# 128-row score passes, exchanged ends of SBUF in the second part, and scalings ordered behind low parts, in a one-core decoder layer

## The chip, the cores and the metric

The kernel runs on 1 core of one Trainium2 chip. Inputs are laid in device memory and one program is launched. The metric is the device time of that program in microseconds (us), the median of several runs. The core's engines are called as in the profile: PE (TensorE, matrix products), PEld (its weight loads), DVE (VectorE), ACT (ScalarE), POOL (GpSimd) and SP (SyncE, which here issues nearly all DMAs).

## The reference

One pre-norm layer over 2048 positions of width 1024, all in float32:

```python
h = rms_norm(x, norm1_g)
proj = h @ w_in                                   # 1024 -> 768 + 1792 columns
q, ka, va = split(proj[..., :768])                # 8 heads of 64; 2 key/value heads
r, k, v, wd, ad, gd = split(token_shift(proj[..., 768:], shift_mu))
att = sliding_window_attention(q, ka, va, sinks)  # window 128, blocks of 128, ALiBi
rw = rwkv7_time_mix(r, k, v, wd, ad, gd, ...)     # 8 heads, recurrent state 64x64 each
x = x + concat([att, rw], -1) @ w_out
h = rms_norm(x, norm2_g)
u = causal_depthwise_conv3(h @ w_gate)            # 1024 -> 2816
x = x + (silu(u) * (h @ w_up)) @ w_down
out = rms_norm(x, final_g)
```

In the attention a block of 128 queries sees the 256 keys of its own block and the one before it: `s = q k^T * 64**-0.5`, minus the slope times the distance, masked, and a softmax with a sink logit per head.

## The kernel before, in words

Every product of two float32 matrices is made of passes in a narrower format (F32R): each operand is split into a high part, copied by ACT, and a low part, which is the operand minus that copy (made by POOL or DVE). `mm3` then issues three passes: high by high, high by low, low by high.

**The first part** (`with ExitStack() as A`) works in 4 blocks of 512 positions and in 4 pairs of heads per block: 16 units, numbered n. One turn of the main loop does several stages for different units at once: `t_prep` and the projections of unit n+2, `t_x` of unit n+1, `chain` (the recurrence) and `t_attn` of unit n, and `t_out` of unit n-1. All PE, ACT and DVE instructions of this part are issued in the order in which the program names them (`in_order`); that order comes from a planner (`tick`, `defer`, `run_until`) with costs and positions in the table `Q`. POOL's and SP's orders are the scheduler's after the first turns.

For `t_x`, a triangular system is solved: `px` makes products on PE, `XB` masks them on DVE, `inv_in` sends them through device memory (`dL`) and back in another layout (`LL`), `subst` makes 31 steps of two DVE instructions each (`Mt` and `M`, woven one at a time between other DVE instructions), `inv_out` brings the result back (`dT`, `TT`), and `merge0` to `merge2` finish it on DVE and PE (`T`, `ph`).

The keys of a block are projected in `ak_done`: ACT writes the high part of each key head g into its own 64 partitions of `kTh`, DVE writes the low part into `kTl` (64 partitions for each head, 128 together), and POOL copies the high part to the other 64 partitions, so that `kTh[:, g]` holds the head's high part twice. A query tile `q{g}` holds the query's high part in one half of the partitions and its low part in the other. In `scores(q2, g)` each of two query blocks has two passes into one PSUM region of 128 by 256:

```python
mm(out=pS[:, e, w0:], lhsT=qg[:, qs], rhs=kTh[:, g, kks]..., start=True, stop=False)
mm(out=pS[:, e, w0:], lhsT=qg[gs, qs], rhs=kTl[gs, kks]..., start=False, stop=True)
```

The first reads 128 partitions, the second 64. There are 4 such calls in each of the 16 units, 64 in all. Each call is followed by the softmax on DVE and ACT (`P`), a transpose on PE (`pT`) and the product with the values (`pO`).

`pw_` makes the decay: one running sum on DVE over 512 positions (`scan`, with the mask `rmask` that starts it again every 64), then exponentials on ACT, of which `E` is used in `writes` one turn later and, in its last column of each chunk, in `chain` two turns later. There are 3 buffers of E.

**The second part** (`with ExitStack() as B`) is traced without that order, but for its first stage. It has three stages:

- O: the output projection (`o_job`, 20 jobs of 24 matmuls), with `cat_load`/`cat_split` for its inputs and `wo_part` for its weights, then the second normalisation, the transposes (`o_tr`) and the operands h2 of the next stage (`combos`). Tiles `r` hold the transposes of positions 1024 and up until they are stored to `h1raw`.
- F: gate and up products in 22 pairs, by a seven-product scheme on 2 by 2 blocks (`quad`, products 1, 6, 7, 5, 2, 4, 3). `unit` splits each weight combination into `uh` and `ul`, six buffers each.
- D: the down product by the same scheme, product by product (`ORDER` 1, 2, 6, 7, 4, 5, 3), 11 steps k of 24 matmuls each. Each step takes three units: two of activations (`ul_a`, low part on POOL) and one of weights (`ul_b`, low part on DVE). `residual` adds x on POOL, `square` sums squares on ACT, `scale_of` makes the factor `rso` on POOL, and `finish` scales and stores: half of the results on DVE while product 3 runs, in its steps k below 8, together with a POOL product `c11 * fgb`.

**Memory.** Pools are stacked from the two ends of each partition of SBUF, in the order in which they are opened; a closed pool gives its bytes to the next on its side, and a tile of the new pool waits until the tiles whose bytes it takes are done, DMAs that read them included. The first tile of a name takes the lowest buffer, the next ones the highest and then downwards. The addresses of the kernel before, in bytes of a partition: first part, constants 928 to 44,800 (with `lgh`, `lgl` at 5,248 to 9,344), operands h 44,800 to 93,952, projection weights to 126,720, scratch `tp` 130,944 to 163,648 (three buffers `t`, which hold `xr`, from 139,136), `pp` to 210,752, attention to 229,248. Second part: from the left `fwp` (three buffers `st` for all loads) 1,504 to 13,792, `rw` 15,072 to 37,600, `op` 37,600 to 111,456 (cath, catl, woh and wol, xn, xt, r), and in their place later `units` 15,072 to 43,744, `fgp`, `hp2`; from the right `h2` 114,656 to 229,344. D's pool `fdp` begins on the left at 43,744.

Of the kernel before, what the change touches and what calls it, by code (L numbers as in the profile page):

```python
# [10 lines left out]
F32 = mybir.dt.float32  # L11
# [72 lines left out]
def hybrid_trunk_kernel(  # L84
# [112 lines left out]
    with ExitStack() as A:  # L197
# [84 lines left out]
        cent = acon.tile([P, P], F32, name="cent")  # L282
        rmask = acon.tile([P, NCH, C], mybir.dt.bfloat16, name="rmask")
        cmask = acon.tile([P, 2, C], mybir.dt.bfloat16, name="cmask")
        cmb = cmask.rearrange("p s t -> p (s t)").unsqueeze(1)
        bias = acon.tile([P, 256], mybir.dt.bfloat16, name="bias")
        kTh = acon.tile([P, 2, 5, P], F32R, name="kTh")
        kTl = acon.tile([P, 5, P], F32R, name="kTl")
        vth = acon.tile([P, 5, P], F32R, name="vth")
        vtl = acon.tile([P, 5, P], F32R, name="vtl")  # L290
        NE = 3
        Es = [acon.tile([P, NCH, C + 1], F32, name=f"E{i}") for i in range(NE)]
# [295 lines left out]
        def t_kv(F, b):  # L588
            def ak_done(ps):
                if b > 0:  # L590
                    gcopy(out=kTh[:, :, 0], in_=f32(kTh[:, :, 4]))
                    gcopy(out=kTl[:, 0], in_=f32(kTl[:, 4]))
                H["kb"] = b
                kh = kTh[:, :, 1:].rearrange("p g n t -> p g (n t)")
                kl = kTl[:, 1:].rearrange("p n t -> p (n t)")
# [24 lines left out]

            return {"ak": ak_done, "av": av_done}, vtr


# [3 lines left out]
        def t_prep(F, n):  # L627
# [4 lines left out]
            S = U[n] = {}  # L632
            E = S["E"] = Es[n % NE]

            def k_done(ps):
# [38 lines left out]
            def pw_():  # L674
# [9 lines left out]
                def go1():  # L684
                    scan(out=sw, data0=rmask.rearrange("p c t -> p (c t)"), data1=sw, initial=0.0, op0=ALU.mult, op1=ALU.add)
# [48 lines left out]
        def t_x(F, n):  # L734
# [84 lines left out]
            def subst():  # L819
                M, LL = S["M"], S["LL"]  # L820
                for i in range(31):
# [61 lines left out]
        def chain(n, fill):  # L883
            b, j = divmod(n, NPAIR)
            u = f"{b}_{j}"
            S = U[n]
            W, SV, XB, Bt, IK, TT, E = S["W"], S["SV"], S["XB"], S["Bt"], S["IK"], S["TT"], S["E"]
# [105 lines left out]
        def t_attn(n):  # L993
# [6 lines left out]
            def scores(q2, g):  # L1000
                def go():
# [13 lines left out]
                    for e in range(2):  # L1015
# [5 lines left out]
                           start=True, stop=False)  # L1021
                        mm(out=pS[:, e, w0:], lhsT=qg[gs, qs], rhs=kTl[gs, kks].rearrange("p n t -> p (n t)"),
                           start=False, stop=True)
# [220 lines left out]
    with ExitStack() as B:  # L1244
        bc = B.enter_context(tc.tile_pool(name="bc", bufs=1, reuse_waits="tile"))
        wp = B.enter_context(tc.tile_pool(name="fwp", bufs=2, reuse_waits="tile"))
        ps_b = B.enter_context(tc.tile_pool(name="ps_b", bufs=8, space=PSUM, reuse_waits="tile"))
        sp_ = B.enter_context(tc.tile_pool(name="fsp", bufs=1, reuse_waits="tile"))
        G = ExitStack()
        h2 = G.enter_context(tc.tile_pool(name="h2", bufs=1, side="right", reuse_waits="tile"))  # L1250

# [3 lines left out]
        def gsub(out, in0, in1):  # L1255
            nc.gpsimd.tensor_tensor(out=out, in0=in0, in1=in1, op=ALU.subtract)  # L1256

# [17 lines left out]
        O = ExitStack()  # L1275
        rw = O.enter_context(tc.tile_pool(name="rw", bufs=1, reuse_waits="tile"))
        op_ = O.enter_context(tc.tile_pool(name="op", bufs=1, reuse_waits="tile"))
        b11, b12 = (h2.tile([P, 4, 512], F32, tag=f"{c}3", name=n) for c, n in (("h", "b11"), ("l", "b12")))
# [170 lines left out]
        F = ExitStack()  # L1449
        up_ = B.enter_context(tc.tile_pool(name="units", bufs=1, reuse_waits="tile"))  # L1450
        gp = F.enter_context(tc.tile_pool(name="fgp", bufs=1, reuse_waits="tile"))
        hp2 = F.enter_context(tc.tile_pool(name="hp2", bufs=1, reuse_waits="tile"))
        NPR = NF // 2
        actc = {p: [dpool.tile([P, NHALF, 512], F32, name=f"actc_{p}_{k}") for k in range(NPR)] for p in PRODS}

        def unit(src, name, lo=gsub, shape=None):
# [6 lines left out]
            act(h_, src, AF.Copy)  # L1463
            lo(l_, src, f32(h_))
            return hi, lw

        def vsub(out, in0, in1):
            nc.vector.tensor_tensor(out=out, in0=in0, in1=in1, op=ALU.subtract)  # L1468

# [263 lines left out]
        def scale_of(j, m):  # L1733
            i = tok[j][m]
            ms = MS[i]
            rs = sp_.tile([P, 1], F32, tag="rso", name=f"rso_{i}", bufs=8)
            gts(out=rs, in0=ms[0], scalar1=ms[1], scalar2=RMS_EPS, op0=ALU.add, op1=ALU.add)
            gtt(out=rs, in0=rs, in1=mhalf[:, 0:1], op=ALU.pow)
            return rs

        def finish(j, m, e, c, rs, scaled=False):
            es = slice(512 * e, 512 * e + 512)
            if scaled:
                act(c, c, AF.Copy, scale=rs)
            else:
                stt(out=c, in0=c, scalar=rs, in1=fgb[:, es], op0=ALU.mult, op1=ALU.mult)
            nc.sync.dma_start(out=out_t[tok[j][m]][:, es], in_=c)
# [5 lines left out]
        for p in ORDER:  # L1753
# [3 lines left out]
            for k in range(NPR):  # L1757
# [76 lines left out]
```

## Time and profile before

| | us |
|---|---|
| median of 3 runs (lowest, highest) | 2703.64 (2700.2, 2708.16) |
| the profiled execution, its time | 2707.62 |
| its span | 2705.9 |
| PE busy in the span | 2568.1 (95%) |
| DVE, POOL, ACT busy | 1722.6, 1461.2, 1284.7 |

The span is from the first to the last instruction of the profiled execution. A busy PE is not PE at its peak, since matmuls are pipelined: the step from the start of one matmul to the start of the next says more than the duration of either. By the names of the tiles the first part ends at about 1244 us, stage O at 1404, stage F at 2261.

### The profile page before, as it was taken

How to read it: one execution, taken by the hardware profiler on the slowest of the kernel's cores; microseconds unless marked ns; L12 is line 12 of the kernel's file. 1: busy time of each engine (PE TensorE's matmuls, PEld its weight loads, DVE VectorE, ACT ScalarE, POOL GpSimd, SP SyncE). 2: the span in 40 equal slices, each digit the busy share in tenths (PEclk: the TensorE clock that was granted, in tenths of full speed). 3: DMA queues.
4: the chain of work that ended last, by engine and by line, in shares of the span. 5: the costliest groups of instructions: out<-in, count | busy, mean ns of one | idle time of the engine just before them, and what ended most of it. 6: DMA issues, size and time to landing. Idle time of an engine off the chain costs nothing.

```text
span 2705.9 us, 42161 instructions
## 1 busy us (share of the span) xinstructions
PE 2568.1 (95%) x15211; PEld 1998.0 (74%) x15211; DVE 1722.6 (64%) x3217; ACT 1284.7 (47%) x2737; POOL 1461.2 (54%) x1356
## 2 busy tenths in 40 slices
PE   7799999999999999998989999999999999999997
PEld 5566766677667766676768788787888888878885
DVE  6577767767677757743756777767676675443343
ACT  5356655655566655643434433345334333343343
POOL 6334443444344434321647778768666665484594
PEclk9899999989999999998999999999999999999998
DMA  4222222222223222335662434545233336742354
GB/s 129 64 63 73 73 73 73 71 59 71 66 64 96 65 65 73 85 110 173 190 206 92 155 135 153 162 165 174 94 98 110 108 113 236 231 141 95 112 176 147
DMA packets 333108, 313.94 MB, mean 116 GB/s; under 512 B 102576, under 2 KB 254274, under 8 KB 332898
## 3 DMA queue, kind: packets, MB, share of 16 engines
q1 hardware_dynamic: 332290, 310.71, 37.3%
q8 instruction: 119, 1.95, 0.3%
q14 instruction: 91, 0.75, 0.1%
q10 hardware_dynamic: 608, 0.53, 0.1%
HBM read 229.26 MB, written 81.92 MB: 115 GB/s over the span
## 4 chain that ended last, share of the span: by engine, by line
PE 63%; DVE 17%; DMA 6%; POOL 5%; issue 5%; ACT 4%; SPq 0%; POOLq 0%; ACTq 0%; DVEq 0%
PE d L104 14%; PE q_g L104 14%; PE q_u L104 12%; DVE M L124 4%; DVE Mt L124 4%; PE poa L104 3%; PE pin_q L104 2%; DMA LL<-dL 2%; PE px L104 2%; PE pc L104 2%; PE pin_k L104 2%; DVE P L124 2%; PE po L104 2%; PE ph L104 1%; PE pS L104 1%
## 5 line engine op out<-in xcount | busy, mean ns | idle before, releaser
L1256 POOL TENSOR_TENSOR ul_a<-sa,uh_a 128x512 fp32r<-128x512 f32 x154 | 208.8, 1361 | 154.6 <-ACT uh_a L110 153.9
L1256 POOL TENSOR_TENSOR ul_u<-s_u,uh_u 128x512 fp32r<-128x512 f32 x154 | 217.2, 1419 | 138.6 <-ACT uh_u L110 138.5
L1256 POOL TENSOR_TENSOR ul_g<-s_g,uh_g 128x512 fp32r<-128x512 f32 x154 | 220.3, 1439 | 56.0 <-ACT uh_g L110 55.9
L104 PE MATMUL q_g<-h2h,uh_g 128*128 128x512 f32 x616 | 242.6, 394 | 6.5 <-DVE u_g L1471 5.9
L104 PE MATMUL q_u<-h2h,uh_u 128*128 128x512 f32 x616 | 240.2, 390 | 2.5 <-DVE ct L1471 2.2
L104 PE MATMUL q_g<-h2l,uh_g 128*128 128x512 f32 x616 | 241.6, 392 | 0.0
L104 PE MATMUL q_g<-h2h,ul_g 128*128 128x512 f32 x616 | 241.3, 392 | 0.3 <-POOL ul_g L1256 0.3
L104 PE MATMUL q_u<-h2h,ul_u 128*128 128x512 f32 x616 | 239.9, 389 | 1.0 <-POOL ul_u L1256 1.0
L104 PE MATMUL q_u<-h2l,uh_u 128*128 128x512 f32 x616 | 239.7, 389 | 0.0
L104 PE MATMUL d<-ul_b,uh_a 128*128 128x512 f32 x616 | 232.4, 391 | 6.7 <-DVE ul_b L1468 6.7
L104 PE MATMUL d<-uh_b,ul_a 128*128 128x512 f32 x616 | 227.5, 391 | 3.5 <-POOL ul_a L1256 3.5
L110 ACT ACTIVATE uh_a<-sa 128x512 fp32r<-128x512 f32 x154 | 97.2, 631 | 235.6 <-PE d L104 128.3
L104 PE MATMUL d<-uh_b,uh_a 128*128 128x512 f32 x616 | 204.1, 389 | 0.0
L110 ACT ACTIVATE uh_u<-s_u 128x512 fp32r<-128x512 f32 x154 | 95.1, 628 | 222.4 <-DVE s_u L1468 116.8
L1468 DVE TENSOR_TENSOR ul_b<-wd,uh_b 128x512 fp32r<-128x512 f32 x55 | 68.1, 1239 | 189.2 <-ACT uh_b L110 183.8
L124 DVE TENSOR_TENSOR Mt<-M,LL 128x60 f32<-128x60 f32 (+24 forms) x496 | 159.8, 322 | 36.8 <-DMA LL<-dL 28.3
L110 ACT ACTIVATE uh_g<-s_g 128x512 fp32r<-128x512 f32 x154 | 95.1, 629 | 185.3 <-PE q_u L104 100.9
L124 DVE TENSOR_TENSOR M<-M,Mt 128x60 f32<-128x60 f32 (+24 forms) x496 | 164.1, 331 | 10.9
L124 DVE SCALAR_TENSOR_TENSOR cc<-g,fcst,cc 128x1024 f32<-128x1024 f32 x88 | 145.5, 1671 | 29.1 <-ACT cc L110 28.4
L104 PEld LDWEIGHTS q_g<-h2h,uh_g 128*128 128x128 f32 x616 | 117.0, 190 | 33.4 <-DVE u_g L1471 7.6
L104 PEld LDWEIGHTS d<-ul_b,uh_a 128*128 128x128 f32 x616 | 116.1, 189 | 31.5 <-DVE ul_b L1468 7.4
L104 PEld LDWEIGHTS d<-uh_b,ul_a 128*128 128x128 f32 x616 | 115.8, 189 | 29.4 <-POOL ul_a L1256 5.5
(370 smaller groups left out, 6988.9 us busy)
## 6 DMA issues: line engine op xcount, KB each, us to landing
sa<-actc SPq DMA_DIRECT2D x77, 512.0 KB
s_g<-in_ffn_w_gate_dram SPq DMA_DIRECT2D x44, 512.0 KB
s_u<-in_ffn_w_up_dram SPq DMA_DIRECT2D x44, 512.0 KB
actc<-cc SPq DMA_DIRECT2D x88, 256.0 KB
actc<-sa SPq DMA_DIRECT2D x66, 256.0 KB
wd<-in_ffn_w_down_dram SPq DMA_DIRECT2D x22, 512.0 KB
s_cat<-catT SPq DMA_DIRECT2D x20, 512.0 KB
x<-in_x_dram SPq DMA_DIRECT2D x16, 512.0 KB
```

The costliest lines, as they stand in the source:

```text
L104: in_order("pe", nc.tensor.matmul(**kw))
L110: in_order("act", nc.scalar.activation(*args, **kw))
L124: in_order("dve", f(*args, **kw))
L1256: nc.gpsimd.tensor_tensor(out=out, in0=in0, in1=in1, op=ALU.subtract)
L1468: nc.vector.tensor_tensor(out=out, in0=in0, in1=in1, op=ALU.subtract)
```

## The change

Four things change. (1) `kTl` gets the shape of `kTh`: each head's low part stands in both halves of the partitions, copied by POOL, and the second pass of `scores` takes all 128 partitions of the query and of `kTl`. (2) To find the room, `rmask` is halved (the running sum becomes two instructions of 256 positions), E has 2 buffers instead of 3, the one column of it that `chain` needs goes into small tiles `eC` (one more ACT instruction per unit), and `Mt` is 76 columns instead of 96. (3) In the second part the pools `fwp`, `rw`, `op`, `units`, `fgp` and `hp2` are stacked from the right end, and `h2` from the left. (4) In D the first instruction of `scale_of`, the DVE scaling in `finish` and the POOL product `c11 * fgb` are each ordered behind the last low part that was traced before them on their engine (an order of issue, not a wait for its end).

```diff
-        rmask = acon.tile([P, NCH, C], mybir.dt.bfloat16, name="rmask")
+        rmask = acon.tile([P, NCH // 2, C], mybir.dt.bfloat16, name="rmask")
-        kTl = acon.tile([P, 5, P], F32R, name="kTl")
+        kTl = acon.tile([P, 2, 5, P], F32R, name="kTl")
-        NE = 3
+        NE = 2
+        eCs = [acon.tile([P, NCH], F32, name=f"eC{i}") for i in range(3)]
...
-                    gcopy(out=kTl[:, 0], in_=f32(kTl[:, 4]))
+                    gcopy(out=kTl[:, :, 0], in_=f32(kTl[:, :, 4]))
...
-                        tt(out=kl[s], in0=ps[s], in1=f32(kh[s, g]), op=ALU.subtract)
+                        tt(out=kl[s, g], in0=ps[s], in1=f32(kh[s, g]), op=ALU.subtract)
                         gcopy(out=kh[hs[1 - g], g], in_=f32(kh[s, g]))
+                        gcopy(out=kl[hs[1 - g], g], in_=f32(kl[s, g]))
...
-                    scan(out=sw, data0=rmask..., data1=sw, initial=0.0, ...)
+                    for h in range(2):
+                        sh = sw[:, h * BLK // 2:(h + 1) * BLK // 2]
+                        scan(out=sh, data0=rmask..., data1=sh, initial=0.0, ...)
...
+                    act(S["eC"], v3(sw)[:, :, C - 1], AF.Exp, scale=-DECAY)
...
-                        Mt = tp.tile([P, 96], F32, tag="Mt", name=f"Mt_{u}_{i}")
+                        Mt = tp.tile([P, 76], F32, tag="Mt", name=f"Mt_{u}_{i}")
...
-                eC = E[:, c, C:C + 1]
+                eC = S["eC"][:, c:c + 1]
...
-                        mm(out=pS[:, e, w0:], lhsT=qg[gs, qs], rhs=kTl[gs, kks]...,
+                        mm(out=pS[:, e, w0:], lhsT=qg[:, qs], rhs=kTl[:, g, kks]...,
...
-        wp = B.enter_context(tc.tile_pool(name="fwp", bufs=2, reuse_waits="tile"))
+        wp = B.enter_context(tc.tile_pool(name="fwp", bufs=2, side="right", reuse_waits="tile"))
-        h2 = G.enter_context(tc.tile_pool(name="h2", bufs=1, side="right", reuse_waits="tile"))
+        h2 = G.enter_context(tc.tile_pool(name="h2", bufs=1, reuse_waits="tile"))
...                       (rw, op, units, fgp, hp2: side="right" as well)
+        last_lo = {}
+        def after_lo(i, eng):
+            if eng in last_lo:
+                tc.add_manual_dep(i.ins, last_lo[eng].ins.name, ... NoSync ..., reason="issue order")
+            return i
...
-            lo(l_, src, f32(h_))
+            last_lo["dve" if lo is vsub else "pool"] = lo(l_, src, f32(h_))
...
-            gts(out=rs, in0=ms[0], scalar1=ms[1], ...)
+            after_lo(nc.gpsimd.tensor_scalar(out=rs, in0=ms[0], scalar1=ms[1], ...), "pool")
...
-                stt(out=c, in0=c, scalar=rs, in1=fgb[:, es], ...)
+                after_lo(nc.vector.scalar_tensor_tensor(out=c, in0=c, scalar=rs, in1=fgb[:, es], ...), "dve")
...
-                    gtt(out=c11[k], in0=c11[k], in1=fgb[:, 0:512], op=ALU.mult)
+                    after_lo(nc.gpsimd.tensor_tensor(out=c11[k], in0=c11[k], in1=fgb[:, 0:512], op=ALU.mult), "pool")
```

## Rows read from the trace of the kernel before

**Rows 1.** Table by stretch: stretch, length, busy us of engines, granted clock, DMA share.

```profile
100.00:1200.00 1100.00, 1048.76 (x8486) 761.89 (x8484) 758.93 (x2123) 640.14 (x1676) 455.42 (x525) 0.97 0.28 73
...
1244.00:1261.00 17.00, 9.84 (x29) 6.40 (x27) 8.21 (x12) 6.09 (x9) 0.00 (x0) 0.70 0.74 230
...
2386.00:2406.00 20.00, 16.55 (x70) 12.50 (x69) 9.31 (x7) 8.26 (x17) 20.00 (x15) 1.00 0.36 114
...
2637.00:2645.00 8.00, 1.35 (x5) 0.83 (x4) 7.64 (x8) 0.00 (x0) 6.23 (x6) 0.73 0.88 311
2645.00:2649.00 4.00, 4.00 (x14) 3.15 (x13) 0.65 (x2) 0.63 (x1) 0.46 (x1) 0.68 0.98 381
```

**Rows 2.** Chain of waits, 100 to 1200 us, shares by line.

```profile
by line: DVE M L124 9.4%; DVE Mt L124 8.9%; PE pin_q L104 6.1%; issue 5.3%; PE px L104 4.7%; PE pc L104 4.7%; PE pin_k L104 4.4%; DMA LL<-dL 4.4%; DVE P L124 4.2%; PE poa L104 3.9%; PE ph L104 3.0%; PE pS L104 2.9%; PE pin_wa L104 2.3%; PE 
```

**Rows 3.** Timeline of PE around one call of scores: start, duration, instruction.

```profile
770.86 0.38 PE L104 MATMUL pS<-kTh,q 128*128 128x256 f32 x1
771.17 0.38 PE L104 MATMUL pS<-kTl,q 64*128 64x256 f32 x1
...
772.11 0.50 PE L104 MATMUL pin_k<-hh,wh_k 128*128 128x512 f32 x1
```

**Rows 4.** Passes that follow others over the same rows: timeline, and a piece of the chain.

```profile
755.77 0.22 PE L104 MATMUL pO<-pth,vtl 128*64 128x128 f32 x1
755.83 0.22 PE L104 MATMUL pO<-pth,vth 128*64 128x128 f32 x1
...
2013.60 13.37 PE q_u L104 x59
```

**Rows 5.** Groups by line: the weight loads of the scores' first pass.

```profile
L104 PEld LDWEIGHTS pS<-kTh,q 128*128 128x128 f32 x128 | 23.9, 186 | 13.1 <-issue 0.7 <-PE pin_r L104 0.7 <-PE pT L107 0.2
```

**Rows 6.** Chain of waits: one unit, then a store in stage O; start, us, what.

```profile
701.89 8.96 DMA LL<-dL
...
711.90 0.20 ACT m L110
...
746.73 2.33 DVE P L124 x2
...
1378.66 5.04 DMA x2d<-xt
```

**Rows 7.** Instructions of kTh and of rmask: ns shortest/median/longest, first and last start.

```profile
L132 POOL CAST kTh<-kTh x11: 390/610/1188, 107.3 to 953.7; 64x512 fp32r<-64x512 f32 x8, 128x256 fp32r<-128x256 f32 x3
...
L124 DVE TENSOR_TENSOR_SCAN sw<-rmask,sw x16: 1204/1218/2308, 33.6 to 1055.2; 128x512 f32<-128x512 bf16 x16
```

**Rows 8.** Timeline from the first part to stage O: SP's queue and PE.

```profile
1233.53 0.38 SPq L1308 DMA_DIRECT2D s_cat<-catT  x1
...
1244.80 0.35 SPq L170 DMA_DIRECT2D x2d<-xr  x1
...
1254.38 0.79 PE L104 MATMUL po<-woh,cath 128*128 128x512 f32 x1 [3.98 <-ACT woh L110]
...
1260.95 0.50 PE L104 MATMUL po<-woh,catl 128*128 128x512 f32 x1 [0.89 <-DVE catl L124]
```

**Rows 9.** Timeline from stage O to stage F: ACT, SP's queue, PE.

```profile
1399.98 0.61 ACT L110 ACTIVATE uh_g<-s_g 128x512 fp32r<-128x512 f32 x1
...
1403.83 1.21 SPq L1369 DMA_DIRECT2D h1raw<-r  x2
...
1407.96 0.50 PE L104 MATMUL q_g<-h2h,uh_g 128*128 128x512 f32 x1 [0.69 <-ACT uh_g L110]
```

**Rows 10.** Timeline of stage D around its two pauses: POOL, PE, DVE, PE.

```profile
2387.76 1.74 POOL L132 TENSOR_TENSOR c<-c,fgb 128x512 f32<-128x512 f32 x1
...
2400.84 1.20 PE L104 MATMUL d<-uh_b,ul_a 128*128 128x512 f32 x4 [1.60 <-POOL ul_a L1256]
...
2642.04 1.75 DVE L124 SCALAR_TENSOR_TENSOR c<-c,rso,fgb 128x512 f32<-128x512 f32 x1
...
2644.44 0.80 PE L104 MATMUL d<-ul_b,uh_a 128*128 128x512 f32 x1 [6.65 <-DVE ul_b L1468]
```

More of the change, by code (lines that the diff above doesn't have):

```diff
@@ L591, in ak_done @@
                     gcopy(out=kTh[:, :, 0], in_=f32(kTh[:, :, 4]))
-                    gcopy(out=kTl[:, 0], in_=f32(kTl[:, 4]))
+                    gcopy(out=kTl[:, :, 0], in_=f32(kTl[:, :, 4]))
                 H["kb"] = b
                 kh = kTh[:, :, 1:].rearrange("p g n t -> p g (n t)")
-                kl = kTl[:, 1:].rearrange("p n t -> p (n t)")
+                kl = kTl[:, :, 1:].rearrange("p g n t -> p g (n t)")
                 for g, s in enumerate(hs):
@@ L633, in t_prep @@
             E = S["E"] = Es[n % NE]
+            S["eC"] = eCs[n % 3]
             def k_done(ps):
@@ L684, in go1 @@
                 def go1():
-                    scan(out=sw, data0=rmask.rearrange("p c t -> p (c t)"), data1=sw, initial=0.0, op0=ALU.mult, op1=ALU.add)
+                    for h in range(2):
+                        sh = sw[:, h * BLK // 2:(h + 1) * BLK // 2]
+                        scan(out=sh, data0=rmask.rearrange("p c t -> p (c t)"), data1=sh, initial=0.0, op0=ALU.mult, op1=ALU.add)
                     defer(Q["e2"], go2, f"e_{u}")
@@ L886, in chain @@
             S = U[n]
-            W, SV, XB, Bt, IK, TT, E = S["W"], S["SV"], S["XB"], S["Bt"], S["IK"], S["TT"], S["E"]
+            W, SV, XB, Bt, IK, TT = S["W"], S["SV"], S["XB"], S["Bt"], S["IK"], S["TT"]
             St = state[j]
@@ L1021, in go @@
                            start=True, stop=False)
-                        mm(out=pS[:, e, w0:], lhsT=qg[gs, qs], rhs=kTl[gs, kks].rearrange("p n t -> p (n t)"),
+                        mm(out=pS[:, e, w0:], lhsT=qg[:, qs], rhs=kTl[:, g, kks].rearrange("p n t -> p (n t)"),
                            start=False, stop=True)
@@ L1255, in gsub @@
         def gsub(out, in0, in1):
-            nc.gpsimd.tensor_tensor(out=out, in0=in0, in1=in1, op=ALU.subtract)
+            return nc.gpsimd.tensor_tensor(out=out, in0=in0, in1=in1, op=ALU.subtract)
         fcst = bc.tile([P, 8 + 4 * NF], F32, name="fcst")
@@ L1275, in hybrid_trunk_kernel @@
         O = ExitStack()
-        rw = O.enter_context(tc.tile_pool(name="rw", bufs=1, reuse_waits="tile"))
-        op_ = O.enter_context(tc.tile_pool(name="op", bufs=1, reuse_waits="tile"))
+        rw = O.enter_context(tc.tile_pool(name="rw", bufs=1, side="right", reuse_waits="tile"))
+        op_ = O.enter_context(tc.tile_pool(name="op", bufs=1, side="right", reuse_waits="tile"))
         b11, b12 = (h2.tile([P, 4, 512], F32, tag=f"{c}3", name=n) for c, n in (("h", "b11"), ("l", "b12")))
@@ L1449, in hybrid_trunk_kernel @@
         F = ExitStack()
-        up_ = B.enter_context(tc.tile_pool(name="units", bufs=1, reuse_waits="tile"))
-        gp = F.enter_context(tc.tile_pool(name="fgp", bufs=1, reuse_waits="tile"))
-        hp2 = F.enter_context(tc.tile_pool(name="hp2", bufs=1, reuse_waits="tile"))
+        up_ = B.enter_context(tc.tile_pool(name="units", bufs=1, side="right", reuse_waits="tile"))
+        gp = F.enter_context(tc.tile_pool(name="fgp", bufs=1, side="right", reuse_waits="tile"))
+        hp2 = F.enter_context(tc.tile_pool(name="hp2", bufs=1, side="right", reuse_waits="tile"))
         NPR = NF // 2
         actc = {p: [dpool.tile([P, NHALF, 512], F32, name=f"actc_{p}_{k}") for k in range(NPR)] for p in PRODS}
+        last_lo = {}
+        def after_lo(i, eng):
+            if eng in last_lo:
+                tc.add_manual_dep(i.ins, last_lo[eng].ins.name,
+                                  mybir.DependencyInfo(mybir.DependencyClass.NoSync, mybir.DependencyReason.DATA),
+                                  reason="issue order")
+            return i
         def unit(src, name, lo=gsub, shape=None):
@@ L1463, in unit @@
             act(h_, src, AF.Copy)
-            lo(l_, src, f32(h_))
+            last_lo["dve" if lo is vsub else "pool"] = lo(l_, src, f32(h_))
             return hi, lw
         def vsub(out, in0, in1):
-            nc.vector.tensor_tensor(out=out, in0=in0, in1=in1, op=ALU.subtract)
+            return nc.vector.tensor_tensor(out=out, in0=in0, in1=in1, op=ALU.subtract)
         def vadd(out, in0, in1):
@@ L1736, in scale_of @@
             rs = sp_.tile([P, 1], F32, tag="rso", name=f"rso_{i}", bufs=8)
-            gts(out=rs, in0=ms[0], scalar1=ms[1], scalar2=RMS_EPS, op0=ALU.add, op1=ALU.add)
+            after_lo(nc.gpsimd.tensor_scalar(out=rs, in0=ms[0], scalar1=ms[1], scalar2=RMS_EPS, op0=ALU.add, op1=ALU.add), "pool")
             gtt(out=rs, in0=rs, in1=mhalf[:, 0:1], op=ALU.pow)
@@ L1745, in finish @@
             else:
-                stt(out=c, in0=c, scalar=rs, in1=fgb[:, es], op0=ALU.mult, op1=ALU.mult)
+                after_lo(nc.vector.scalar_tensor_tensor(out=c, in0=c, scalar=rs, in1=fgb[:, es], op0=ALU.mult, op1=ALU.mult), "dve")
             nc.sync.dma_start(out=out_t[tok[j][m]][:, es], in_=c)
```

## The prediction, made before the changed kernel was run

> **What bounds the kernel now.** I read the table by stretch first [rows 1]. In the first part PE is busy 1048.76 of 1100 us at a granted clock of 0.97, so it looks bound by PE; a second look is needed because the chain of waits [rows 2] says something else. There the two DVE instructions of the substitution, Mt and M, hold 18.3% of the same stretch, the transfer LL 4.4%, and the scores 2.9%. One unit shows how both can be true [rows 6]: LL lands at 701.89 + 8.96 = 710.85, and the chain then runs on DVE until 749.06, where the softmax P is ready. That is 47 us of a unit of about 69 (16 units in some 1100 us) in which PE is busy but its time decides nothing. Then I looked at the timeline where the changed passes are [rows 3], at passes that keep their rows [rows 4], at the joints between stages [rows 8, 9], and at the two places in stage D where PE pauses [rows 10].
>
> **Scores, on PE alone.** A call has four passes, from 770.86 to 772.11: 1.25 us, 0.31 a step, whichever way the rows change, 128 to 64 or back [rows 3]. Passes that keep their rows step by 0.06 us at 128 columns (755.77 to 755.83) and by 13.37/59 = 0.227 us at 512 [rows 4]. No row shows 256 columns with rows kept; on the line between these two it is 0.06 + 0.167/3 = 0.116, say 0.12. Bounds: at least 0.06, and at most 0.31, no gain. So each step saves 0.19. Three steps lie inside a call, 0.57; the fourth is saved only when the next pass also reads 128 rows, 0.76 then. I take 0.66. For 64 calls that is 42 us of PE.
>
> The 0.19 rests on the next weights being loaded while a pass still runs. The load takes 186 ns [rows 5], and at a step of 60 ns it must overlap the pass before it. The Trainium skill says otherwise (TensorE: Matmul & The Clock Gate, section "The mechanism"): a weight load overlaps matmuls in flight only when its row group differs. By that rule the change would gain nothing; the trace of pO, rows unchanged, disagrees.
>
> **What the end gets of it.** Scores hold 2.9% of 1100 us of the chain, 31.9 us [rows 2], or 31.9/1.25 = 25.5 of the 64 calls. Only these can move the end: 25.5 x 0.66 = 16.8 us. The rest falls beside the substitution on DVE, which does not get shorter. A path that is almost as long stands behind in every unit, so I take 70%, 11.8.
>
> **What the first part gets in addition.** POOL: two more copies of 64x512 per block, 8 in all, at the 0.61 us of its likes for kTh [rows 7], 4.9 us; the three carried copies get twice as wide. ACT: 16 instructions of 8 columns, at 0.20 as the small one at 711.90 [rows 6], 3.2 us. DVE: each running sum of 1.218 us [rows 7] becomes two; nothing at least, 0.2 more at most for a second start, so up to 3.2 us. Together under 12 us on three engines; what lies on the chain of it I put at 2. Queued behind POOL's copies are the low parts wl; the scores that need kTl come in the next turn, by the table of positions, which covers the copies. The E buffers cost nothing: E is read one turn after it is written, and the third buffer is replaced by eC. Sum for the first part: 11.8 - 2 = about 10; bounds 0 and 40.
>
> **From the first part to stage O.** PE is busy 9.84 of 17 us at clock 0.70 from 1244 to 1261 [rows 1]; its 29 passes are worth 29 x 0.227 = 6.6, so 10.4 us are lost. The reason is in the addresses: st, cath and woh lie over lgh and over h, which the last projections read to the end. SP could issue the first load s_cat at 1233.53 only, and PE waits for woh at 1254.38 and for catl at 1260.95 [rows 8]. Exchanged, st lies at 217,056 and up, over the attention's tiles, which are done earlier, and the loads can go at once. woh and wol lie from 137,056, over the tiles t. The last t holds xr, stored from 1244.80 [rows 8], and keeps wol of k = 1 and woh of k = 2 waiting until that store lands. A store of this size took 5.04 us on a loaded chain [rows 6]; I take half. So PE, done with poa at about 1244, stops after one k until about 1248, and again some 2 us for the fourth weight load, whose buffer comes free with that wol. I count 4.5 us saved, bounds 1 and 10.4.
>
> **From stage O to stage F.** Here the exchange costs. op is 73,856 bytes and units 28,672: op begins at 217,056 - 22,528 - 73,856 = 120,672, its tiles r stand 65,664 further, and the second of them begins at 188,384. units also begin at 217,056 - 28,672 = 188,384. So the first uh takes the bytes of the second r, and by the order of buffers (lowest, then from the highest down) that is the r written last. Before, the first uh_g ran at 1399.98. Now it waits for the last store of r, issued about 1404.7 [rows 9], plus 2.5: 1407.2. ACT takes 0.6, then POOL up to 1.74 for its low part (the length of another product of this shape [rows 10]), ten more passes 2.3, and the next product, which began at 1407.96 [rows 9], begins about 1411.7. DVE's combinations wait for that low part as well, because they overwrite its source. I take a loss of 3.7; bounds 0 (another buffer is taken) and 6 (a store of 5.04).
>
> **Stage D.** At 2386 to 2406 POOL is busy 20.00 of 20 us and PE only 16.55 [rows 1]: PE waits for ul_a behind residuals and behind c11 * fgb, 1.74 us each [rows 10], which nobody needs before the end. Tied behind the low parts of product 3 they leave, 8 x 1.74 = 13.9 us of POOL, and the 3.45 us should go. At 2637 to 2645 DVE is busy 7.64 us in 8 instructions; they are scalings, and ul_b stands behind them, so PE waits 6.65 us [rows 1, 10]. After it the clock is 0.68 for 4 us [rows 1]: 0.64 of them at half speed, 1.3 us lost. Tied, one pair of scalings comes per step of 24 x 0.227 = 5.45 us. The sum is 3.45 + 6.65 + 1.3 = 11.4; bounds 5 (the residuals alone keep the first pause, POOL delays a little) and 12. fgb and wd now lie over h2, all read by 2261, and none is needed before product 6.
>
> **Sum.** 10 + 4.5 - 3.7 + 11.4 = 22.2. The profiled execution took 2707.62, 1.7 more than its span, and lies 4 above the median of the runs; 2703.64 - 22.2 = 2681.
>
> **Rivals.**
> - PE bounds the whole first part, as its 95% suggests. Then all 42 - 2 count: 30 us more, 2651. Against it: the 38 us on DVE in one unit [rows 6] and the share of M and Mt [rows 2].
> - The first part gives nothing, since the substitution on DVE decides every unit. 12 remain, 2691.
> - The changed passes step no faster: the next weights are not loaded during a pass over the same rows, so a step is the columns, half of 0.227, plus the 186 ns of a load [rows 4, 5], 0.30 against 0.31. Again 12 remain, 2691. Against it: the step of 0.06. The rule of the Trainium skill named above (TensorE: Matmul & The Clock Gate, section "The mechanism") would have it so.
> - POOL sets the pace of product 3: per step two ul_a and one c11 * fgb at 1.74 are 5.2 us, and the factors rso come on top, against 5.45. One microsecond too much in 8 steps eats the 8 us won at 2637: 2689.
> - Slower: the freed time of PE turns into pauses, and the granted clock falls after them. The price of one such fall is the 1.3 us after the pause of 6.65 [rows 1]. With the first part's gain gone and 12 us left, it decides from 10 falls on; at two in each of 16 units, 42 us, the time is 2733. For it: PE's waits there are short now and will grow. Against it: 0.97 over 1100 us now.
>
> **How the numbers follow.** Chances: the forecast 0.57 (2670 to 2689 by its own bounds), PE all along 0.08, nothing in the first part 0.19, steps no faster 0.02, POOL's pace 0.08, slower 0.06. The range of 8 in 10 is 2663 to 2695: below it lies the first rival, above it the last and a part of the second with the dearer stage F. A measurement tells a change of 0.3%, 8 us, from none. Faster by more: 0.57 + 0.08 + 0.07 and 0.12 of the 0.21 of the two that leave 12, that is 0.84; within, the rest of these, 0.10; slower 0.06.
>
> **What would show it.** Right: four passes of pS with steps near 0.12 and, between 100 and 1200, PE's waits grown by more than 20 us; the first part shorter by some 10 and not 40; po waiting near 1248 minus that; the first uh_g released by the store to h1raw; c11 * fgb after product 3 began, no PE pause in D beyond 1 us. Wrong: steps of pS near 0.31 (the overlap), a first part shorter by 25 or more (the chain read wrongly), uh_g at its old distance (the buffer order), POOL at 100% in product 3.

## The result, and the profile of the changed kernel

The changed kernel takes 2686.37 us (median of 6 runs, 2683.90 to 2690.20), the kernel before beside it 2703.55 (2697.08 to 2711.34): a ratio of 0.9933, interval 0.9912 to 0.9954, by which it is 18 us less (17 by the medians). The forecast was 2681 in a range of 2663 to 2695, with 0.84 on "faster by more than 0.3%". The profiled execution took 2685.55 us, its span is 2683.8, 22.1 less than the span of before.

Where these 22.1 us lie is read from five marks of PE's timeline: the first po, the last po, the first q_g, the first d, and the end of the span.

| stretch | before | after | difference | forecast |
|---|---|---|---|---|
| start to first po | 1243.9 | 1230.3 | -13.6 | -10 |
| first to last po (stage O) | 151.4 | 150.5 | -0.9 | -4.5 |
| last po to first q_g | 8.3 | 12.9 | +4.6 | +3.7 |
| first q_g to first d (stage F) | 857.1 | 855.1 | -2.0 | 0 |
| first d to the end (stage D) | 445.2 | 435.0 | -10.2 | -11.4 |

The first view is the table by stretch, with the columns of [rows 1]: the first part, the joint to stage O, the place of the former pause at product 6, and product 3.

```profile
100.00:1200.00 1100.00, 1025.90 (x8551) 760.48 (x8550) 770.35 (x2154) 644.65 (x1702) 460.26 (x534) 0.96 0.29 74
...
1230.30:1246.60 16.30, 10.22 (x25) 6.68 (x24) 7.79 (x11) 5.03 (x8) 0.00 (x0) 0.69 0.68 216
...
2380.00:2400.00 20.00, 20.00 (x90) 16.55 (x89) 10.66 (x8) 8.06 (x15) 15.57 (x12) 1.00 0.46 144
...
2611.00:2656.00 45.00, 44.54 (x195) 35.95 (x194) 29.77 (x23) 15.68 (x30) 45.00 (x40) 1.00 0.48 164
```

PE is idle for 74.1 us of the 1100 where it was 51.2 [rows 1]: 22.9 us more, and the first part ends only 13.6 us earlier. At the joint the clock is as low as before. At product 6 the pauses are gone. In product 3 POOL is busy 45.00 of 45.00 us and PE still 44.54.

The timeline of PE at the same call of scores as in [rows 3]:

```profile
761.87 0.33 PE L104 MATMUL pc<-Pt,TT 64*64 64x64 f32 x4
762.13 0.39 PE L104 MATMUL pS<-kTh,q 128*128 128x256 f32 x1
762.35 0.28 PE L104 MATMUL pS<-kTl,q 128*128 128x256 f32 x1
762.47 0.28 PE L104 MATMUL pS<-kTh,q 128*128 128x256 f32 x1
762.58 0.28 PE L104 MATMUL pS<-kTl,q 128*128 128x256 f32 x1
762.70 0.39 PE L104 MATMUL pin_k<-hh,wh_k 128*128 128x512 f32 x1
```

Four passes take 0.57 us (762.13 to 762.70) instead of 1.25. Three of the steps are 0.11 to 0.12; the first, of the pass that follows pc over 64 rows, is 0.22. The load of weights takes 188 ns, 186 before [rows 5]. Its place shows what changed; PEld's timeline at the second pass of the call, first in the kernel before, then in the changed one:

```profile
771.17 0.18 PEld L104 LDWEIGHTS pS<-kTl,q 64*128 64x128 f32 x1
```
```profile
762.23 0.19 PEld L104 LDWEIGHTS pS<-kTl,q 128*128 128x128 f32 x1
```

Before, the load starts at the time at which its pass is put (771.17); now it starts 0.12 us ahead of it (762.23 against 762.35), while the pass before it runs.

What PE waited for between 100 and 1200 us, from the table of waits (total, times, longest):

```profile
PE pT L107 <- DVE P L124: 21.5, 19, 3.7
PE pc L104 <- ACT Pt L110: 16.9, 16, 2.8
PE pc L104 <- ACT Ut L110: 9.9, 12, 1.9
```

Before, these three were 19.9, 6.4 and 3.8 us: PE arrives earlier at the chain of the state (pc, Pt, Ut) and waits there.

At the joint to stage O, first PE, then ACT, then SP's queue, then DVE, from their timelines:

```profile
1230.30 0.40 PE L104 MATMUL po<-woh,cath 128*128 128x512 f32 x1
1234.07 0.80 PE L104 MATMUL po<-wol,cath 128*128 128x512 f32 x1 [3.38 <-DVE wol L124]
1234.66 0.63 PE L104 MATMUL po<-woh,catl 128*128 128x512 f32 x1
...
1241.61 0.49 PE L104 MATMUL po<-woh,cath 128*128 128x512 f32 x1 [2.47 <-ACT woh L110]
...
1243.63 0.63 PE L104 MATMUL po<-woh,catl 128*128 128x512 f32 x1
1244.06 0.63 PE L104 MATMUL po<-woh,cath 128*128 128x512 f32 x1
...
1246.60 0.25 PE L107 MATMUL pfc<-ident,frow 96*128 96x96 f32 x1
```
```profile
1233.31 1.67 ACT L110 ACTIVATE woh<-swo 128x512 fp32r<-128x512 f32 x3 [6.28 <-DMA x2d<-xr]
1240.92 1.15 ACT L110 ACTIVATE woh<-swo 128x512 fp32r<-128x512 f32 x2 [5.95 <-DMA swo<-in_w_out_dram]
```
```profile
1214.82 1.05 SPq L1304 DMA_DIRECT2D swo<-in_w_out_dram  x2
...
1225.77 5.77 SPq L170 DMA_DIRECT2D x2d<-xr  x2
...
1234.09 0.38 SPq L1304 DMA_DIRECT2D swo<-in_w_out_dram  x1
```
```profile
1231.11 1.22 DVE L124 TENSOR_TENSOR catl<-s_cat,cath 128x1024 fp32r<-128x1024 f32 x1
```

There are two stops, as forecast: 3.38 us for wol behind the store of xr, after one pass and not after one k, and 2.47 for the weights of k = 4, which come with the third load and not with the fourth. After the first of them passes step by 0.43 us instead of 0.227, after the second from 1.6 us on (1243.21): the clock is at its lower level, 1.2 of 2.4 GHz (0.69 over the stretch). The first two loads of weights now go at 1214.82, where s_cat, ahead of them, went at 1233.53 before [rows 8]: so far the exchange does what was forecast. The third load is issued at 1234.09, behind the last store of xr in SP's queue, and lands 6.8 us later. Another place in the queue alone would have won less than 2 us: of the three buffers `st` only that of s_cat can be the one that it takes, the other two being still in use, and that one comes free when catl is made, at 1232.3.

Going into stage F, ACT and PE:

```profile
1393.01 0.63 ACT L110 ACTIVATE uh_g<-s_g 128x512 fp32r<-128x512 f32 x1 [7.19 <-DMA h1raw<-r]
```
```profile
1393.69 0.79 PE L104 MATMUL q_g<-h2h,uh_g 128*128 128x512 f32 x1 [4.02 <-ACT uh_g L110]
...
1395.04 0.79 PE L104 MATMUL q_g<-h2h,ul_g 128*128 128x512 f32 x1
1395.63 0.63 PE L104 MATMUL q_g<-h2h,uh_g 128*128 128x512 f32 x1
...
1399.47 0.63 PE L104 MATMUL q_g<-h2h,uh_g 128*128 128x512 f32 x1
```

The first uh_g is released by the store to h1raw, as forecast. In stage D, the instructions of c on POOL, the last of PE's waits, and two instructions of POOL and DVE in product 3:

```profile
L1793 POOL TENSOR_TENSOR c<-c,fgb x8: 1280/1289/1295, 2612.2 to 2654.0; 128x512 f32<-128x512 f32 x8
```
```profile
2648.03 0.50 PE L104 MATMUL d<-ul_b,uh_a 128*128 128x512 f32 x1 [0.23 <-DVE ul_b L1483]
...
2661.05 0.50 PE L104 MATMUL d<-ul_b,uh_a 128*128 128x512 f32 x1 [1.30 <-DVE ul_b L1483]
```
```profile
2616.97 1.25 POOL L1752 TENSOR_SCALAR rso<-ms,ms 128x1 f32<-128x1 f32 x1
```
```profile
2655.84 1.78 DVE L1761 SCALAR_TENSOR_TENSOR c<-c,rso,fgb 128x512 f32<-128x512 f32 x1 [1.90 <-POOL rso L132]
```

The eight c11 * fgb, which began at 2384.4 before, begin at 2612.2, within product 3. Of the 6.65 us [rows 10] a wait of 1.30 is left, and two of 0.23.

### The profile page after: what moved, and what is told of

Read it like the earlier page. It is cut to its first block, busy times and chain, and to the rows that moved or that the text cites. A ratio compares the mean times of both kernels' runs of the same rounds, so it can differ in the third digit from the quotient of the medians.

```text
span 2683.8 us, 42227 instructions
## 1 busy us (share of the span) xinstructions
PE 2534.4 (94%) x15211; PEld 1988.0 (74%) x15211; DVE 1740.1 (65%) x3232; ACT 1285.3 (48%) x2753; POOL 1469.0 (55%) x1364
## 4 chain that ended last, share of the span: by engine, by line
PE 62%; DVE 17%; DMA 7%; ACT 5%; issue 4%; POOL 4%; SPq 0%; POOLq 0%; ACTq 0%; DVEq 0%
PE q_g L104 14%; PE d L104 14%; PE q_u L104 13%; DVE M L124 4%; DVE Mt L124 4%; PE pin_q L104 3%; PE poa L104 3%; DMA LL<-dL 3%; PE px L104 2%; PE po L104 2%; PE pc L104 2%; DVE P L124 2%; PE pin_k L104 1%; PE ph L104 1%; PE pO L104 1%
## 5 line engine op out<-in xcount | busy, mean ns | idle before, releaser
L124 DVE TENSOR_TENSOR M<-M,Mt 128x60 f32<-128x60 f32 (+24 forms) x496 | 155.7, 314 | 10.8
L104 PEld LDWEIGHTS q_u<-h2h,uh_u 128*128 128x128 f32 x616 | 115.6, 188 | 27.2 <-DVE ct L1486 1.4
```

What stands on the lines that cost most here:

```text
L104: in_order("pe", nc.tensor.matmul(**kw))
L124: in_order("dve", f(*args, **kw))
```

## The experiments

Ratios are to runs of the kernel before on the same chip, with the interval. One us is 0.0004; differences of two ratios are worked out with 2705 us. The first part varies by itself: in traces of three kernels whose first part is that of before, the first po comes at 1239.2, 1243.9 and 1244.4; in six with that of the changed kernel, between 1225.7 and 1246.2. So the first part is judged by ratios, the joints and stages behind it by marks. These vary too: stage O takes 148.6 to 153.1 us in the six kernels with its buffers as before, stage F 855.1 to 857.7 in the eleven kernels that leave cc in its place, e10 aside, and 859.6 in e10.

### The first part, the exchange, the scalings: one at a time

**e1: the first part alone.** The changed kernel with the seven pools back on their former sides and without `after_lo`.

> The kernel before with the first part of the change alone (128-row scores, the low parts copied into both halves, the shorter mask, eC, two E buffers); the buffers of the second part lie as before and no scaling is tied. If the terms of my sum stand by themselves, the first part ends 10 to 14 us earlier and nothing else moves: 2690 to 2694 us. Rival: of the 13.6 us that the trace of the changed kernel shows there, some 5 arise at the very end of the first part, where before a wait for Y was followed by passes at half clock, and belong to the exchanged buffers or to chance: 2695 to 2697. The first q_g should then come 10 to 14 us earlier than at 1403.57, with no wait of PE for uh_g there beyond 1 us.

2695.90 us, the time of the rival; ratio 0.9969 (0.9950 to 0.9988): 8.4 us less, 3.2 to 13.5. From the last po to the first q_g it takes 8.2 us, as before. The first part's share is nearer the forecast 10 than the 13.6 of the trace.

**e2: the exchange alone**, on the kernel before:
```
-wp = B.enter_context(tc.tile_pool(name="fwp", bufs=2, reuse_waits="tile"))
+wp = B.enter_context(tc.tile_pool(name="fwp", bufs=2, side="right", reuse_waits="tile"))
...                        (h2 to the left; rw, op, units, fgp, hp2 to the right)
```


> The kernel before with the exchange of ends alone. By my sum it saves 4.5 us from the first part to stage O and costs 3.7 going into stage F: 2703. By the trace of the changed kernel it saves less than 1 us at the first joint and costs 4.4 at the second, 2 of which come back within stage F: 2704 to 2707. PE should wait about 4 us for the first uh_g, released by the store to h1raw.

2708.99 us, 2 to 6 more than expected; ratio 1.0008 (0.9990 to 1.0026). Stage O takes 152.1 us (151.4 before), the way to the first q_g 12.6. PE's timeline:

```profile
1409.08 0.80 PE L104 MATMUL q_g<-h2h,uh_g 128*128 128x512 f32 x1 [4.03 <-ACT uh_g L110]
```

By itself the exchange gains nothing and costs 4 us at the second joint.

**e3: the tied scalings alone**, on the kernel before: `after_lo`, its three uses, and `last_lo`, which `unit` writes.

> The kernel before with the scalings tied behind the low parts and nothing else. By my sum stage D loses 11.4 us, by the trace of the changed kernel 10.2: 2692 to 2694. Rival: POOL, busy without a break in product 3, falls behind by a microsecond or more a step and PE waits for it at the end: 2700 or more. The wait of 6.65 us for ul_b and the three at product 6 should be gone.

2690.61 us, ratio 0.9944 (0.9922 to 0.9966): 15 us less, 9 to 21. Stage D takes 436.7 us instead of 445.2, 8.5 less; what the ratio has beyond that is not assigned (in this trace the first po comes 4.7 us earlier, at 1239.2). The waits of PE for ul_b sum to 3.1 us, longest 1.4, where the largest was 6.65.

**e9: the added work alone.** The kernel of e1 with the passes over the low parts on 64 rows:
```
-mm(out=pS[:, e, w0:], lhsT=qg[:, qs], rhs=kTl[:, g, kks]...
+mm(out=pS[:, e, w0:], lhsT=qg[gs, qs], rhs=kTl[gs, g, kks]...
```


> The kernel before with all that the first part of the change adds (copies of the low parts, split running sum, eC, two E buffers) while the passes over the low parts stay on 64 rows; ends of SBUF and scalings as before. My prediction put the added work at 2 us: 2707. By the run with the changed kernel and 64 rows, which gave back 13 of 18 us where the exchange and the tied scalings alone should keep 12, it is 4 to 8 us: 2709 to 2713. If it costs nothing, the time is that of the kernel before.

2712.68 us, ratio 1.0026 (1.0006 to 1.0047): 7 us more, 1.6 to 12.7. The difference to e1, the rows of the passes alone, is 0.0057, 15 us (8 to 23). So the 8.4 of e1 are 15 won and 7 lost.

**e4: the changed kernel with 64 rows**, the same line.

> The changed kernel with the passes over the low parts of the keys put back on 64 rows; the copies, eC, the split sums and everything else stay. If the rows of the passes are what shortens the first part, it is as long as before plus some 2 us for the work added: 2699 to 2702, and the steps within a call of scores are again 0.31. Rival: the shorter first part comes from the rest (eC, fewer buffers, another order of work), and the passes give nothing because they lie beside the substitution: 2686 to 2688.

2700.09 us, ratio 0.9981 (0.9963 to 0.9999): 13 us (6 to 21) of the 18 are gone with the rows. In its trace the steps are 0.31 and 0.32 again:

```profile
771.06 0.38 PE L104 MATMUL pS<-kTl,q 64*128 64x256 f32 x1
771.38 0.38 PE L104 MATMUL pS<-kTh,q 128*128 128x256 f32 x1
771.69 0.38 PE L104 MATMUL pS<-kTl,q 64*128 64x256 f32 x1
```

### What a pass costs, and how much of it counts

**e5: the order high, high, low, low**, on the kernel before. Two sums of one bank are open at a time here, and the scores are not those of the reference; only the time is read.

> The kernel before with the four passes of a call of scores in another order: both over the high parts (128 rows), then both over the low parts (64 rows); nothing is added or copied. If it is the change of rows that makes a step 0.31 instead of 0.12, two of the steps in a call get short, 0.38 us, 24 us of PE over 64 calls; the same share of it as in the changed kernel (13.6 of 42) reaches the end: about 8 us, 2694 to 2698. Rival: a pass over 64 rows is slow by itself; then one step gets short, 12 us of PE, about 4 us at the end: 2699 to 2701.

2697.11 us, ratio 0.9966 (0.9949 to 0.9983): 9 us less. A call in PE's timeline:

```profile
764.11 0.50 PE L104 MATMUL pS<-kTh,q 128*128 128x256 f32 x2
764.55 0.50 PE L104 MATMUL pS<-kTl,q 64*128 64x256 f32 x2
764.97 0.50 PE L104 MATMUL pin_k<-hh,wh_k 128*128 128x512 f32 x1
```

0.86 us for four passes. Two passes over 64 rows take 0.42, two over 128 rows 0.44. A pass over 64 rows is not slow; the change of rows is, either way.

**e6: each low pass three times**, in the changed kernel.

> The changed kernel with each pass over the low parts of the keys made three times instead of once (the scores then hold the low part's product three times); 256 more passes of 0.116 us, 29.7 us of PE. If PE bounds the whole first part, all of it is added: 2716. If only the calls on the chain count (25.5 of 64, and a path nearly as long behind), a third: 2694 to 2698. If nothing of it counts, 2686 to 2688.

2707.36 us, ratio 0.9997 (0.9978 to 1.0015), 0.0064 over the changed kernel: 17 us, 10 to 25, of the 29.7 that PE has more to do. More than the third expected, less than all. By the medians, work added to PE counts for a larger share (17 of 30) than work taken away (15 of 43 by e9 and 64 calls of 0.68); the intervals overlap, so this is not shown. The chain's share of the calls, 25.5 of 64, would be 12 of 30, inside the interval.

**e10: the order high, low, low, high, with the tied scalings**, on the kernel before; no copies, no exchange:
```
+for i in range(4):
+    e = i // 2
...
+    if i in (0, 3):
+        mm(out=pS[:, e, w0:], lhsT=qg[:, qs], rhs=kTh[:, g, kks]..., start=i == 0, stop=i == 3)
+    else:
+        mm(out=pS[:, e, w0:], lhsT=qg[gs, qs], rhs=kTl[gs, kks]..., start=i == 2, stop=i == 1)
```


> The kernel before with the scalings tied, and the four passes of a call of scores in the order high, low, low, high: two changes of rows per call where there were four, counting the one into the next pass; no copies, no added work, ends of SBUF as before. With the tied scalings alone the time was 14 us under that of the kernel before. If each change of rows costs 0.19 us, another 24 us of PE go, of which 8 to 10 reach the end: 2682 to 2686, as fast as the whole change. Rival: the accumulation that begins on 64 rows, or the wait of the next product for the last pass, costs what the order saves: 2690 to 2693.

2685.22 us, ratio 0.9918 (0.9894 to 0.9943): as fast as the whole change, without its copies and without the exchange. Over e3, the tied scalings alone, that is 0.0026, 7 us (-2 to 16): what the order adds there is not told from nothing by these runs; e5 is the run that shows a gain by order. PE's timeline:

```profile
763.10 0.39 PE L104 MATMUL pS<-kTh,q 128*128 128x256 f32 x1
763.42 0.50 PE L104 MATMUL pS<-kTl,q 64*128 64x256 f32 x2
763.85 0.38 PE L104 MATMUL pS<-kTh,q 128*128 128x256 f32 x1
764.07 0.39 PE L104 MATMUL pin_k<-hh,wh_k 128*128 128x512 f32 x1
```

0.97 us a call: two changes of rows inside it where there were four with the one into the next pass, by the order alone.

### The joints

**e7: r over the tiles t, cc first in stage F**, in the changed kernel:
```
 cats[0] = cat_split(*OJ[0], st0[0])
+op_.tile([P, 512], F32, tag="r", name="r_place", bufs=4)
...
 gp = F.enter_context(tc.tile_pool(name="fgp", ...))
+gp.tile([P, HALF], F32, tag="cc", name="cc_place", bufs=4)
```


> The changed kernel with the buffers r put over the tiles t of the first part (below woh) and the buffers cc first among those of stage F, so that neither woh and wol lie over the last xr, nor the first uh over the last r. If the overlap of uh with r is what delays stage F, uh_g no longer waits for the store to h1raw, the first q_g follows the last transposes within 2 us and the end comes 2 to 4 us earlier; the pause of 3.4 us for the first wol goes as well, but the loads of the later weights, which stand behind the store of the last xr in SP's queue, still decide when job 0 ends. Together 2680 to 2684. Rival: the time is given back inside stage F, at the first waits for u_g, and at the later weights: 2685 to 2687.

2693.85 us, ratio 0.9951 (0.9929 to 0.9972): not faster. The marks say why. From the last po to the first q_g it takes 8.3 us, so the overlap of uh and r is what cost 4.6. The joint to stage O did not change: pfc comes 16.3 us after the first po, as in the changed kernel, so the place of woh does not decide there. Stage F takes 863.6 us instead of 855.1. There the mean of a DVE instruction of pairs of cc, which stands beside POOL's work, got longer (groups by line; busy in us, mean in ns), the changed kernel first, then e7:

```profile
L1486 DVE TENSOR_TENSOR sa<-cc,cc 128x512 f32<-128x512 f32 x21 | 37.0, 1761 | 59.2 <-POOL cc L1695 59.2
```
```profile
L1488 DVE TENSOR_TENSOR sa<-cc,cc 128x512 f32<-128x512 f32 x21 | 47.0, 2238 | 59.4 <-POOL cc L1697 59.4
```

The median stays at 1.76 us and the longest take 4.27. PE waits 10.5 us for u_g instead of 5.9. What of the new addresses does this is not settled.

**e11: r and xt in each other's place**, nothing else:
```
 frow = ffn_consts()
+op_.tile([P, 512], F32, tag="r", name="r_place", bufs=4)
 x_load(0)
```


> The changed kernel with the buffers r put in the place of xt and xt in that of r, nothing else moved. The first uh then lies over xt, which is read earlier. If the store of the last r is what delays stage F, the first q_g follows the last po after 8.3 us instead of 12.9, and stage F takes the 855 to 857 us that it took: 4 to 5 us less, 2681 to 2683. In the run where r lay over the tiles t and cc was moved too, the first q_g came early and stage F took 7 to 8 us longer; if that was the moved cc, it does not come back here; if it is the earlier start that changes what DVE and POOL do at the same time, it does: 2686 to 2690.

2681.18 us, ratio 0.9918 (0.9888 to 0.9948). The first uh_g (ACT's timeline) now follows xn:

```profile
1382.74 0.63 ACT L110 ACTIVATE uh_g<-s_g 128x512 fp32r<-128x512 f32 x1 [1.80 <-DVE xn L124]
```

The first q_g comes 8.5 us after the last po, stage F takes 856.7 us. So the loss in e7 does not come from the earlier start. Of what e7 moved, cc is the likelier cause, since the instruction that got longer reads it; e7 also put r elsewhere than e11 did, so this is argued.

**e8: r and cc as in e7, and the loads ahead of the stores.** The first cat tile and the last weights of job 0 go into b22, the first catl to POOL:
```
-s = wp.tile([P, D], F32, tag="st", name=f"s_cat_{i}_{e}", bufs=3)
+s = b22[:, 2:]... if (i, e) == OJ[0] else wp.tile(...)
...
+s = stage[e] = b22[:, :2] if (e, k) == (1, 6) else wp.tile(...)
```


> As the one before, and the first cat tile and the last pair of weights for job 0 are loaded into b22, which is still unused, so that all four loads of weights can be issued ahead of the last stores of xr; the first catl is made on POOL, which is idle there. If the place of the loads in SP's queue is what costs 10 us at this joint, job 0 follows the last poa with pauses of under 2 us, some 5 to 9 us are won there, and the end comes at 2673 to 2678. Rival: the cat tile of job 1, loaded after them, is late next and keeps most of it: 2679 to 2682.

2690.19 us, far above the 2673 to 2678 expected and above the rival; ratio 0.9941 (0.9921 to 0.9962). pfc comes 6.9 us after the first po instead of 16.3. Then PE's timeline shows what is late next:

```profile
1241.37 0.25 PE L107 MATMUL pfc<-ident,frow 96*128 96x96 f32 x1
1245.53 0.80 PE L104 MATMUL po<-woh,cath 128*128 128x512 f32 x1 [3.91 <-ACT cath L110]
```

The cat tile of job 1 costs 3.91 us, and half speed follows; at the last po 3.9 of the 9.4 us are left, and stage F (860.5) takes 5, as in e7. The edit did three things at once, the place of the loads in the queue, the buffer that they need and the engine of the first catl; by the wait for s_cat's buffer above, the queue alone had less than 2 us to give.

**e12: e11 and the loads**, with the cat tile of job 1 in b21 and the first catl on POOL:

> As the one before, with the first two cat tiles and the last pair of weights of job 0 loaded into b21 and b22, which are unused until the third job, and the first catl made on POOL. The loads then stand ahead of the last stores of xr in SP's queue. woh and wol still lie over the last xr, so the first wait for wol of some 3 us stays. If the loads are what keeps job 0 and job 1, job 0's 24 passes end 8 to 10 us after the first instead of 16.3, job 1 does not wait for its cat tile, and the end comes 5 to 8 us before that of the run above: 2674 to 2678. Rival: the tiles of the jobs behind are late next and take most of it back: 2679 to 2683.

2680.78 us, ratio 0.9898 (0.9871 to 0.9926), the lowest ratio; the time is that of the rival, not the 2674 to 2678 forecast. PE's timeline:

```profile
1229.79 0.79 PE L104 MATMUL po<-wol,cath 128*128 128x512 f32 x1 [3.38 <-DVE wol L124]
...
1237.68 0.25 PE L107 MATMUL pfc<-ident,frow 96*128 96x96 f32 x1
...
1248.73 1.04 PE L107 MATMUL pt<-ident,xn 128*128 128x128 f32 x8
```

From the first po (1226.0) pfc takes 11.7 us (8 to 10 expected), stage O 146.4 instead of 150.5. The one stop left is the overlap of wol with the last xr; half speed behind it lasts for 12 passes. By ratio it is not told apart from e11 (0.9918); by the marks, 4 us.

## Why the prediction was right, and where its sum was not

- **Steps of the scores**: 0.12 forecast, 0.11 to 0.12 in the trace for three of four, 0.22 for the first; a call is 0.68 us shorter, 0.66 forecast. Right. The rule that a load of weights overlaps matmuls in flight only when its row group differs (the Trainium skill, TensorE: Matmul & The Clock Gate, section "The mechanism") does not hold for these passes: loads of 188 ns lie beside passes over the same 128 rows that follow each other every 0.12 us. The same section also allows a load ahead of its turn into a background weight buffer; with that the trace agrees.
- **What of it reaches the end**: 11.8 of 42 us forecast from the chain; e9 to e1 say 15, the changed kernel to e4 says 13. So the chain of waits is nearer than PE's 95%, by which all 42 would count. PE's idle time grew by 22.9 us, over the 20 named. Both intervals (8 to 23, 6 to 21) hold the 11.8 and the uncut 16.8: whether the cut to 70% was right is not shown.
- **Added work**: 2 forecast, 7 measured (1.6 to 12.7, e9). By the medians this and the last term are both too small and cancel in the sum, 10 against the 8.4 of e1: the near hit of the two together is luck. Which of copies, split sums, eC and the third E buffer costs it, no run separates.
- **First part to stage O**: this step failed. "I count 4.5 us saved" came to 0.9. The stops were sized right, some 4 us until 1248 and some 2 for the fourth load: 3.38 and 2.47. But I let PE run at full speed between them. The 24 passes up to pfc, worth 24 x 0.227 = 5.4 us, take 16.3; 10.9 are lost, of which 6.1 are the waits (3.38, 2.47 and one of 0.23) and 4.8 are half speed. The forecast left 10.4 - 4.5 = 5.9, the waits alone. The 10.4 us lost before contain half speed too (clock 0.70 [rows 1]); what I left of them after the change did not. The reason of the second stop was also another: not the fourth load behind wol, but the third, which needs the buffer of the first cat tile and stands behind the store of xr. Moving woh alone does nothing (e7), moving the loads, their buffers and catl does (e8, e12); which of the three is not separated.
- **Stage O to stage F**: mechanism right; e2 shows it with the exchange alone, e11 removes it. The first uh_g begins 12.2 us after the last po instead of 4.7, 7.5 later, 7.2 forecast. The size is right in part by luck. At the mark that the forecast named, the start of the next product, the loss is 6.0 and not 3.7 (1399.47 is 18.7 us behind the last po, 1407.96 [rows 9] was 12.7), since the ten passes ahead of it take 4.4 us at half speed where I had 2.3. Part of this comes back within stage F: from the last po to the first d the four kernels with the exchange and r where the change puts it (after, e2, e4, e6) take 868.0 to 869.5 us, five with the ends of before 865.4 to 865.9 (e10 868.6, not explained), 2 to 4 us in the end.
- **Stage D**: 11.4 forecast, 10.2 in the trace and 8.5 in e3. What is missing are the waits for ul_b that remain, 1.8 us in the trace and 3.1 in e3. They come by way of POOL: the rival of POOL's pace happened, without its price. A step of product 3 takes POOL 5.98 us (one c11 * fgb at 2612.20, the next at 2618.18), PE 5.45. The products cost less than the 1.74 each that I had, 4.3 us for the two ul_a and c11 * fgb; the factors rso cost more, 1.8, of which 1.25 is one instruction of 128x1 that takes 0.30 at the end (2668.87). DVE's scaling waits 1.90 us for rso (2655.84), and ul_b stands behind it. Eight steps fall back by 4.2 us; PE works on units made ahead, so waits of 0.23, 0.23 and 1.30 are all that shows. The last is over the 1 us that I had named as a limit. I had also named a POOL at 100% as a sign against the forecast; it was none, since the lead of the units was not in that sentence.
- **The rivals**: "PE bounds the whole first part" is excluded by e1 against e9 and by e4 (15 and 13 of 43 us, at most 23), "the first part gives nothing" by the interval of e1, "no faster steps" by the timeline. The clock hardly fell: 0.96 over the 1100 us, 0.95 to 0.97 in the six traces with this first part.

By these marks the change sums to -8.4 - 0.9 + 4.6 - 2.0 - 10.2 = -16.9, beside 18 by the ratio. The forecast's 22.2 was 4 to 5 us too much, 3.6 of them at the one joint. The 2.0 of stage F lie near its variation.

## What to carry to other kernels

Count changes of the row group between passes before paying for wider operands: putting equal passes next to each other bought 9 us without any added work (e5), where the copies bought 8.4 (e1); e10 has such an order with the right sums, and there its gain over e3 is 7 us, -2 to 16. When a stop of PE is costed, add the passes after it that run at half speed, once for every stop that remains. When buffers change ends, list for each new neighbour the last store of the old and the first write of the new tile, and for each load what stands ahead of it in its queue and whose buffer it takes: here one joint gained nothing and the other lost 4.6 us, and by the marks moving one tag won that back (e11).

## What the hardware showed that was not expected

- A change between 64 and 128 rows costs about 0.19 us at 256 columns in either direction: 0.31 against 0.12 a step where the rows change at every pass (before, e4), and 0.39 us less for two changes fewer in a call (1.25 to 0.86, e5). About half of it falls on the pass ahead of a change and half on the pass behind: a first step of 0.22 behind pc in the changed kernel, 0.22 for the last pass in e10. The Trainium skill (TensorEngine Tiling (Array Packing), section "Key Properties") says that changing the tiling mode drains TensorE, without a figure. A price at each change agrees with that; that it is a drain, no row shows.
- The same scaling on DVE, by rso and fgb, takes 1.78 us (c at 2655.84) while POOL makes ul_a of 128x512, and 0.74 to 0.76 at the end (cu, from 2670.32), where POOL's instructions are 128x1. A busy POOL alone does not do it: in product 3 ul_b, with two inputs as well, takes 0.68 (2617.45) beside rso. The Trainium skill (GPSIMD Engine Reference, section "1. Specifications") has POOL's access to SBUF shared with VectorE, with contention when a DVE instruction has two inputs in SBUF; these rows agree, and sa<-cc,cc does too, 0.69 in a gap of POOL (2251.51) and 1.76 in the median. It goes both ways: rso on POOL takes 1.25 us (2616.97) where the scaling and ul_b run on DVE, and 0.30 (2668.87) beside cu<-d,cu, whose d is in PSUM.
